# The opening of a decoder layer's kernel: constant matmuls before the first operands, first affines in halves, sums of operands behind the next modulation

## The chip, the cores and the metric

The kernel runs on one core of a Trainium2 chip. The metric is the device time of one launch in microseconds; three runs of the kernel before have a median of 1798.16 us.

## The reference, cut to what matters

One layer of a decoder with D = S = 1024: two gated feed-forward blocks (macaron halves) around a token mix, each behind a modulation by a vector c and before a LayerNorm. The change lies in the first block:

```python
silu_c = jax.nn.silu(c)
mods = silu_c @ w_ada[l] + b_ada[l]
sh1, sc1, g1, sh2, sc2, g2, sh3, sc3, g3 = [m[:, None, :] for m in jnp.split(mods, N_MODS, axis=-1)]
h = modulate(x, sh1, sc1)          # x * (1 + scale) + shift
y = swiglu(h, ffn1_w_gate[l], ffn1_w_up[l], ffn1_w_down[l])
```

The feed-forward width is 2816, so gate and up have 22 blocks of 128 columns each.

## The kernel before, in words

All matrices are f32. A product of f32 accuracy is made of three matmuls on halves (`split`, L101 to L103): ScalarE casts the operand to a high half (L102), VectorE subtracts it and leaves the low half (L103); `mm3` (L105 to L109) multiplies high by high, high by low, and low by high, each matmul 128 columns of weights against 512 columns.

The opening is `start_ffn1` (L561 to L633). The modulated input is made in eight chunks d of 128 features, transposed, 1024 tokens wide. `fetch(d)` loads two 128x1024 pieces of the modulation's weights (rows of adaT) and one chunk of x. `modulation(d)` (L579) reduces each piece against silu(c) on VectorE (`ada_mul`, L120: one reduction of 128x1024 and a short read of its accumulator) into a shift and a scale per feature. ScalarE applies them to the whole chunk (L597, 128x1024), then both token halves are split. TensorE multiplies the chunk at once with the weights of the first two column blocks of gate and of up, eight banks of PSUM wide (24 matmuls per chunk); these are the groups mm, mm, mm, o and y, y, tp, tp. After the last chunk ScalarE and VectorE evict the eight banks (L626 to L628: a Tanh, a scalar_tensor_tensor and a multiplication, four on VectorE for each of two row tiles).

The further column blocks are made by Strassen's scheme in the form of Winograd: seven products instead of eight (`product`, L280), over sums of the operands. T1 to T4 are sums of the input's quarters (`t_sum`, L221, on VectorE; `t_split`, L240), made of chunks d - 4 and d once chunk d is there, so in the rounds d of 4 to 7. Weights are loaded, summed and split in `w_ops` (L248). The seven products of gate, then of up, run in `gate_up` (L347).

A scheduler of the framework sets the order in which the instructions stand on each engine when the program is built: it starts what it holds to be ready earliest, within the order of the program. Each engine then works strictly in that order and waits on semaphores. `tc.issue_after(ins)` is a block whose instructions the scheduler places behind the instruction named. Buffers of SBUF are rings by tag (`RING`), and a load waits on SyncE's queue until a buffer is free. SyncE issues all loads and stores.

Of the kernel before, what the change touches and what calls it, by code (L numbers as in the profile page):

```python
# [1 line left out]

# [30 lines left out]
TAIL = 2  # L33
LOOK = 1
SECOND = 3
EARLY = 3
RATIO = 1.25
RATIO2 = 0.3
# [8 lines left out]
def layer_kernel(ctx, tc, xT, x, c, adaT, adab, wg1, wu1, wd1, wqk, wv1, wv2, bf, sinks,  # L47
# [16 lines left out]
    def st(tag, shape, dt=F32):  # L64
        assert 4 * math.prod(shape[1:]) <= RING[tag][1], (tag, shape)
        return mk(sb, shape, dt, tag, RING[tag][0])
# [7 lines left out]
    def psum(tag):  # L74
        return mk(ps, [P, HT], F32, tag, BANK[tag])
# [21 lines left out]
    def mod_b(m):  # L97
        return bcol[:, m * KD:(m + 1) * KD]
# [12 lines left out]
    def halves(t):  # L111
        return [t[:, :HT], t[:, HT:]]
# [7 lines left out]
    def ada_mul(w, j):  # L120
        m = j // KD
        s = 0.125 if m in (2, 8) else 0.5
        V.tensor_tensor_reduce(w, w, silu, scale=s, scalar=bcol[:, j:j + 1], op0=ALU.mult,
                               op1=ALU.add, accum_out=modc[:, j:j + 1])

    def ada_block(m, d):
        j = m * KD + d
# [112 lines left out]
    def t_split(n, ops, d):  # L240
        if n not in ops:
            ops[n] = htiles()
        split(ops[n][0][:, d], ops[n][1][:, d], ops["s" + n, d])
# [285 lines left out]
    for n in range(2):  # L529
# [2 lines left out]
        th = st("t", [P, HT])  # L532
        A.activation(th, silu[:, cs], AF.Tanh, scale=0.5)
        V.scalar_tensor_tensor(silu[:, cs], th, 1.0, silu[:, cs], op0=ALU.add, op1=ALU.mult)
    DMA.dma_start(bcol, adab)
    for m in (1, 4, 7, 2, 5, 8):
        V.tensor_scalar(mod_b(m), mod_b(m), 1.0, 0.25 if m in (2, 8) else 1.0, op0=ALU.add, op1=ALU.mult)

    def weight_std(w, c, tag):

# [20 lines left out]
    def start_ffn1():  # L561
        ops = {}
        hd = []
        blk = {}
        w0 = w1 = None
        p0 = [[psum("mm"), psum("mm")], [psum("mm"), psum("o")]]
        p1 = [[psum("y"), psum("y")], [psum("tp"), psum("tp")]]
        ada = {}

        def fetch(d):  # L570
            if d < KD:
                ada[d] = st("h", [P, 2, D])
                for m in range(2):
                    j = m * KD + d
                    DMA.dma_start(ada[d][:, m], adaT[j * P:(j + 1) * P, :])
                hd.append(st("z" if d < 4 else "q", [P, S]))
                DMA.dma_start(hd[d], xT[d * P:(d + 1) * P, :])

        def modulation(d):  # L579
            if d < KD:  # L580
                for m in range(2):
                    ada_mul(ada[d][:, m], m * KD + d)

        fetch(0)
        modulation(0)
        for d in range(KD):
            t = hd[d]
            if d:
                fetch(d + 1)
            if d in (0, SECOND):  # L590
                if d == 0:
                    w0 = [weight_std(wg1, 0, "w"), weight_std(wu1, 0, "w")]
                for _, load in w0:
                    load(d > 0)
            if d == 0:
                fetch(1)
            A.activation(t, t, AF.Identity, bias=modc[:, d:d + 1], scale=modc[:, KD + d:KD + d + 1])  # L597
            if d % 4 == 0:
                for hf in range(2):
                    blk[d // 4, hf] = htiles()  # L600
            for hf in range(2):
                hi, lo = blk[d // 4, hf]
                split(hi[:, d % 4], lo[:, d % 4], halves(t)[hf])
            if d in (0, SECOND):
                if d == 0:
                    w1 = [weight_std(wg1, 1, "w"), weight_std(wu1, 1, "t")]
                for _, load in w1:
                    load(d > 0)
            modulation(d + 1)
            for w, p in ((w0, p0), (w1, p1)):  # L610
                for q in range(2):
                    for hf in range(2):
                        hi, lo = blk[d // 4, hf]
                        mm3(p[q][hf], *w[q][0][d], hi[:, d % 4], lo[:, d % 4], d == 0, d == KD - 1)
            if d >= 4:
                for n in ("T1", "T2", "T3", "T4"):
                    t_sum(n, hd, ops, d - 4, V)
                for n in ("T1", "T2"):
                    t_split(n, ops, d - 4)
        ops["B11"], ops["B21"], ops["B22"] = blk[0, 0], blk[1, 0], blk[1, 1]  # L620
        a = []
        for j, p in enumerate((p0, p1)):
            a.append(st("z", [P, S]))
            for hf in range(2):
                t = halves(a[j])[hf]
                A.activation(t, p[0][hf], AF.Tanh, scale=0.5)  # L626
                V.scalar_tensor_tensor(t, t, 1.0, p[0][hf], op0=ALU.add, op1=ALU.mult)
                V.tensor_tensor(t, t, p[1][hf], ALU.mult)  # L628
        wo = w_ops(wg1, 2)
        for n in ("T3", "T4"):  # L630
            for d in range(4):
                t_split(n, ops, d)
        return ops, wo, a  # L633
# [7 lines left out]
    DMA.dma_start(gaincol, gain)  # L641
    DMA.dma_start(bfb, bf[0].partition_broadcast(P))
    DMA.dma_start(sinkb, sinks[0].partition_broadcast(P))
    V.memset(ones, 1.0)
    V.memset(nhalf, -0.5)
    V.tensor_scalar(nsink, sinkb, -1.0, None, op0=ALU.mult)

    rest = [(m, d) for m in range(2, 9) for d in range(KD)]
# [779 lines left out]
```

## Time and profile before

| | us |
|---|---|
| median of three runs | 1798.16 |
| lowest, highest | 1797.49, 1800.76 |
| the profiled execution | 1802.0 |
| its span, first to last instruction | 1800.2 |

PE is TensorE, PEld its weight loads, DVE VectorE, ACT ScalarE, SP SyncE. A row of a timeline says when an instruction starts, how long it takes from start to result, its line, operation and shape, and in brackets how long the engine had been idle before it and what ended that. Instructions overlap on an engine: the next one can start before the one before has its result, so what an instruction takes of the engine's time is read from the distance of starts. [...]

### The profile page before, as it was taken

Reading aid. Unit: us, or ns where it says so; the run is one execution under the profiler, and the core shown is the slowest. Engines: PE = TensorE matmul, PEld = TensorE weight load, DVE = VectorE, ACT = ScalarE, POOL = GpSimd, SP = SyncE. Lnnn points to the kernel's source line nnn. Section 1 sums busy time; section 2 is a strip of 40 time slices with the busy share of each in tenths; the row PEclk is TensorE's granted clock in tenths of the full one; section 3 lists DMA queues with packets and bytes.
Section 4 is the critical chain, followed back from the end, with each engine's and each line's share of the span. In section 5 each row is a group of like instructions: output and inputs, shape, how many; then the busy total and the mean of one; then the engine's idle time right before and its main releaser. Section 6 shows DMA issues by size and latency. Waiting matters only on the chain.

```text
span 1800.2 us, 23514 instructions
## 1 busy us (share of the span) xinstructions
PE 1749.5 (97%) x8114; PEld 1439.8 (80%) x8114; DVE 1520.0 (84%) x2759; ACT 772.3 (43%) x1481; POOL 23.1 (1%) x32
## 2 busy tenths in 40 slices
PE   7999999999999999999999989999999999999997
PEld 5788888888888889777777768678888888888885
DVE  7999999999696796378878887999788887789788
ACT  5433333333544452376556641543233333344472
POOL 0000000000000000000000000000000000000000
PEclk9999999999999999999999999999999999999999
DMA  9355565557944336755677862333224233593452
GB/s 366 122 193 180 192 200 183 185 175 250 324 122 146 94 102 224 228 154 161 187 212 214 231 221 85 130 111 135 94 94 137 92 105 100 189 314 112 136 163 82
DMA packets 147047, 303.44 MB, mean 169 GB/s; under 512 B 15384, under 2 KB 29296, under 8 KB 146928
## 3 DMA queue, kind: packets, MB, share of 16 engines
q1 hardware_dynamic: 146928, 301.94, 51.9%
q8 instruction: 64, 1.05, 0.3%
q14 instruction: 55, 0.45, 0.1%
HBM read 224.17 MB, written 77.71 MB: 168 GB/s over the span
## 4 chain that ended last, share of the span: by engine, by line
PE 80%; DVE 11%; ACT 3%; DMA 3%; issue 2%; POOL 0%; SPq 0%; ACTq 0%; DVEq 0%; POOLq 0%
PE y L107 11%; PE y L108 11%; PE y L109 11%; PE mm L107 9%; PE mm L109 9%; PE mm L108 9%; PE o L107 3%; PE o L108 3%; PE o L109 3%; DVE h L103 2%; PE tp L107 2%; PE tp L109 2%; PE tp L108 2%; DVE w L103 1%; PE tp L1140 1%
## 5 line engine op out<-in xcount | busy, mean ns | idle before, releaser
L102 ACT CAST w<-u 128x512 fp32r<-128x512 f32 x303 | 186.4, 622 | 387.6 <-PE y L109 156.9
L107 PE MATMUL y<-h,w 128*128 128x512 f32 x728 | 287.8, 395 | 5.1 <-ACT h L102 2.1
L108 PE MATMUL y<-h,w 128*128 128x512 f32 x728 | 286.1, 393 | 0.0
L109 PE MATMUL y<-h,w 128*128 128x512 f32 x728 | 285.6, 393 | 0.0
L103 DVE TENSOR_TENSOR w<-u,w 128x512 fp32r<-128x512 f32 x303 | 206.1, 685 | 25.0 <-ACT w L102 23.9
L107 PE MATMUL mm<-h,w 128*128 128x512 f32 x528 | 207.2, 393 | 18.6 <-ACT h L102 15.5
L108 PE MATMUL mm<-h,w 128*128 128x512 f32 x528 | 207.2, 393 | 0.3 <-DVE h L103 0.2
L109 PE MATMUL mm<-h,w 128*128 128x512 f32 x528 | 206.8, 392 | 0.0
L107 PEld LDWEIGHTS y<-h,w 128*128 128x128 f32 x728 | 137.2, 188 | 33.7 <-ACT h L102 2.5
L109 PEld LDWEIGHTS y<-h,w 128*128 128x128 f32 x728 | 137.1, 188 | 26.9
L108 PEld LDWEIGHTS y<-h,w 128*128 128x128 f32 x728 | 137.1, 188 | 25.8
L102 ACT CAST w<-t 128x512 fp32r<-128x512 f32 x106 | 65.5, 621 | 190.8 <-PE mm L109 68.8
L107 PEld LDWEIGHTS mm<-h,w 128*128 128x128 f32 x528 | 99.8, 189 | 40.7 <-ACT h L102 15.9
L108 PEld LDWEIGHTS mm<-h,w 128*128 128x128 f32 x528 | 100.2, 190 | 22.0 <-DVE h L103 1.5
L109 PEld LDWEIGHTS mm<-h,w 128*128 128x128 f32 x528 | 99.9, 189 | 21.5 <-DVE w L103 0.8
L102 ACT CAST z<-u 128x512 fp32r<-128x512 f32 x88 | 54.7, 622 | 93.1 <-PE y L109 59.8
L103 DVE TENSOR_TENSOR t<-tp,t 128x512 fp32r<-128x512 f32 (+1 forms) x126 | 72.9, 586 | 21.6 <-ACT t L102 20.3
L103 DVE TENSOR_TENSOR z<-u,z 128x512 fp32r<-128x512 f32 x88 | 60.1, 686 | 26.2 <-ACT z L102 26.1
L102 ACT CAST t<-tp 128x512 fp32r<-128x512 f32 (+1 forms) x126 | 62.3, 502 | 46.2 <-PE tp L1140 45.3
L102 ACT CAST w<-h 128x512 fp32r<-128x512 f32 x111 | 68.3, 617 | 31.8 <-DMA h<-in_wd 13.3
L103 DVE TENSOR_TENSOR w<-h,w 128x512 fp32r<-128x512 f32 x111 | 75.7, 685 | 5.3 <-ACT w L102 5.2
L103 DVE TENSOR_TENSOR w<-t,w 128x512 fp32r<-128x512 f32 x106 | 72.6, 687 | 1.6 <-ACT w L102 1.1
(347 smaller groups left out, 3909.3 us busy)
## 6 DMA issues: line engine op xcount, KB each, us to landing
u<-aT SPq DMA_DIRECT2D x154, 256.0 KB, 2.8
q<-in_adaT SPq DMA_DIRECT2D x56, 512.0 KB, 3.4
u<-in_wg SPq DMA_DIRECT2D x92, 256.0 KB, 3.0
u<-in_wu SPq DMA_DIRECT2D x90, 256.0 KB, 2.8
aT<-z SPq DMA_DIRECT2D x44, 512.0 KB, 3.4
h<-in_wd SPq DMA_DIRECT2D x88, 256.0 KB, 5.4
qkd<-w SPq DMA_DIRECT2D x26, 512.0 KB, 3.5
aT<-b SPq DMA_DIRECT2D x22, 512.0 KB, 4.2
```

Of the source, the lines that this page charges most:

```text
L102: A.copy(hi, src)
L103: V.tensor_tensor(lo, src, hi.bitcast(F32), ALU.subtract)
L107: T.matmul(o, lh, rh, start=start, stop=False, skip_group_check=more)
L108: T.matmul(o, lh, rl, start=False, stop=False, skip_group_check=more)
L109: T.matmul(o, ll, rh, start=False, stop=stop, skip_group_check=more)
L1140: T.transpose(pt[:, tok(i - q0)], sps[i][:, tok(j)], ident)
```

## The change

1. 28 matmuls of the constant `ones` with itself (128x128, f32) into a bank that nobody reads stand at the start of `start_ffn1`; the memsets of `ones` and `nhalf` move to the front for it, and the banks of the groups are asked for behind it.
2. The affine of chunks 0 and 1 is issued as two halves of 128x512.
3. The four sums and the two splits of a round d of 4 to 7 are placed behind the second reduction of `modulation(d + 1)`; after the last chunk there is none.
4. The load of the bias `bcol` is issued behind the first piece of the modulation's weights; of the six additions to it the one that the first scale needs stays ahead of the first modulation, and five are issued at the end of round 1.

```diff
@@ -1,3 +1,4 @@
+import contextlib
 import math
 
 import concourse.bass as bass
@@ -33,6 +34,7 @@
 TAIL = 2
 LOOK = 1
 SECOND = 3
+WARM = 28
 EARLY = 3
 RATIO = 1.25
 RATIO2 = 0.3
@@ -120,8 +122,8 @@
     def ada_mul(w, j):
         m = j // KD
         s = 0.125 if m in (2, 8) else 0.5
-        V.tensor_tensor_reduce(w, w, silu, scale=s, scalar=bcol[:, j:j + 1], op0=ALU.mult,
-                               op1=ALU.add, accum_out=modc[:, j:j + 1])
+        return V.tensor_tensor_reduce(w, w, silu, scale=s, scalar=bcol[:, j:j + 1], op0=ALU.mult,
+                                      op1=ALU.add, accum_out=modc[:, j:j + 1])
 
     def ada_block(m, d):
         j = m * KD + d
@@ -532,9 +534,13 @@
         th = st("t", [P, HT])
         A.activation(th, silu[:, cs], AF.Tanh, scale=0.5)
         V.scalar_tensor_tensor(silu[:, cs], th, 1.0, silu[:, cs], op0=ALU.add, op1=ALU.mult)
-    DMA.dma_start(bcol, adab)
-    for m in (1, 4, 7, 2, 5, 8):
-        V.tensor_scalar(mod_b(m), mod_b(m), 1.0, 0.25 if m in (2, 8) else 1.0, op0=ALU.add, op1=ALU.mult)
+
+    def bcol_add(ms):
+        for m in ms:
+            V.tensor_scalar(mod_b(m), mod_b(m), 1.0, 0.25 if m in (2, 8) else 1.0, op0=ALU.add, op1=ALU.mult)
+
+    V.memset(ones, 1.0)
+    V.memset(nhalf, -0.5)
 
     def weight_std(w, c, tag):
 
@@ -563,8 +569,6 @@
         hd = []
         blk = {}
         w0 = w1 = None
-        p0 = [[psum("mm"), psum("mm")], [psum("mm"), psum("o")]]
-        p1 = [[psum("y"), psum("y")], [psum("tp"), psum("tp")]]
         ada = {}
 
         def fetch(d):
@@ -573,16 +577,24 @@
                 for m in range(2):
                     j = m * KD + d
                     DMA.dma_start(ada[d][:, m], adaT[j * P:(j + 1) * P, :])
+                    if d + m == 0:
+                        DMA.dma_start(bcol, adab)
                 hd.append(st("z" if d < 4 else "q", [P, S]))
                 DMA.dma_start(hd[d], xT[d * P:(d + 1) * P, :])
 
         def modulation(d):
             if d < KD:
-                for m in range(2):
-                    ada_mul(ada[d][:, m], m * KD + d)
-
+                return [ada_mul(ada[d][:, m], m * KD + d) for m in range(2)][1]
+
+
+        warm = psum("o")
+        for _ in range(WARM):
+            T.matmul(warm[:, :P], ones, ones, start=True, stop=True)
         fetch(0)
+        bcol_add((1,))
         modulation(0)
+        p0 = [[psum("mm"), psum("mm")], [psum("mm"), psum("o")]]
+        p1 = [[psum("y"), psum("y")], [psum("tp"), psum("tp")]]
         for d in range(KD):
             t = hd[d]
             if d:
@@ -594,7 +606,8 @@
                     load(d > 0)
             if d == 0:
                 fetch(1)
-            A.activation(t, t, AF.Identity, bias=modc[:, d:d + 1], scale=modc[:, KD + d:KD + d + 1])
+            for hs in [t] if d > 1 else halves(t):
+                A.activation(hs, hs, AF.Identity, bias=modc[:, d:d + 1], scale=modc[:, KD + d:KD + d + 1])
             if d % 4 == 0:
                 for hf in range(2):
                     blk[d // 4, hf] = htiles()
@@ -606,17 +619,20 @@
                     w1 = [weight_std(wg1, 1, "w"), weight_std(wu1, 1, "t")]
                 for _, load in w1:
                     load(d > 0)
-            modulation(d + 1)
+            done = modulation(d + 1)
             for w, p in ((w0, p0), (w1, p1)):
                 for q in range(2):
                     for hf in range(2):
                         hi, lo = blk[d // 4, hf]
                         mm3(p[q][hf], *w[q][0][d], hi[:, d % 4], lo[:, d % 4], d == 0, d == KD - 1)
             if d >= 4:
-                for n in ("T1", "T2", "T3", "T4"):
-                    t_sum(n, hd, ops, d - 4, V)
-                for n in ("T1", "T2"):
-                    t_split(n, ops, d - 4)
+                with tc.issue_after(done.ins) if done else contextlib.nullcontext():
+                    for n in ("T1", "T2", "T3", "T4"):
+                        t_sum(n, hd, ops, d - 4, V)
+                    for n in ("T1", "T2"):
+                        t_split(n, ops, d - 4)
+            if d == 1:
+                bcol_add((4, 7, 2, 5, 8))
         ops["B11"], ops["B21"], ops["B22"] = blk[0, 0], blk[1, 0], blk[1, 1]
         a = []
         for j, p in enumerate((p0, p1)):
@@ -641,8 +657,6 @@
     DMA.dma_start(gaincol, gain)
     DMA.dma_start(bfb, bf[0].partition_broadcast(P))
     DMA.dma_start(sinkb, sinks[0].partition_broadcast(P))
-    V.memset(ones, 1.0)
-    V.memset(nhalf, -0.5)
     V.tensor_scalar(nsink, sinkb, -1.0, None, op0=ALU.mult)
 
     rest = [(m, d) for m in range(2, 9) for d in range(KD)]
```

The order of the instructions shows what the scheduler makes of it.

**ScalarE, chunks 0 and 1.** In round 1 the weights w and t are those of the second pair of blocks, and z is the chunk of x. Before:

```order
L597 ACTIVATE z_105<-z_105,modc 128x1024
L102 CAST w_109<-u_113 128x512
L102 CAST h_127<-z_105 128x512
L102 CAST w_111<-u_117 128x512
L102 CAST h_129<-z_105 128x512
L597 ACTIVATE z_124<-z_124,modc 128x1024
L102 CAST w_135<-u_137 128x512
L102 CAST t_143<-u_141 128x512
```

And now:

```order
L610 ACTIVATE z_122<-z_122,modc 128x512 x2
L104 CAST w_135<-u_139 128x512
L104 CAST h_154<-z_122 128x512
L104 CAST w_137<-u_143 128x512
L104 CAST h_156<-z_122 128x512
L610 ACTIVATE z_150<-z_150,modc 128x512
L104 CAST w_162<-u_164 128x512
L104 CAST t_170<-u_168 128x512
L610 ACTIVATE z_150<-z_150,modc 128x512
L104 CAST h_154<-z_150 128x512
```

In chunk 0 both halves still stand ahead of the first cast; in chunk 1 the casts of the second weights stand between the halves.

**VectorE, around the modulation of chunk 6** (its weights are h_352 before and h_385 now; lines L231, L234, L237 before and L230 to L239 now are sums, L103 and L105 low halves). Before:

```order
L231 TENSOR_TENSOR t_389<-q_302,z_124 128x512
L103 TENSOR_TENSOR h_349<-t_340,h_348 128x512
L103 TENSOR_TENSOR h_306<-q_302,h_305 128x512
L103 TENSOR_TENSOR h_308<-q_302,h_307 128x512
L234 TENSOR_TENSOR z_124<-q_302,z_124 128x512
L237 TENSOR_TENSOR q_302<-q_302,t_389 128x512
L103 TENSOR_TENSOR h_345<-z_124,h_344 128x512
L103 TENSOR_TENSOR h_349<-t_389,h_348 128x512
L123 ISA h_352,modc<-h_352,b_75,bcol 128x1024
L123 ISA modc 128x1
L123 ISA h_352,modc<-h_352,b_75,bcol 128x1024
L123 ISA modc 128x1
```

And now:

```order
L233 TENSOR_TENSOR t_373<-q_281,z_122 128x512
L236 TENSOR_TENSOR z_122<-q_281,z_122 128x512
L239 TENSOR_TENSOR q_281<-q_281,t_373 128x512
L105 TENSOR_TENSOR h_378<-z_122,h_377 128x512
L105 TENSOR_TENSOR h_339<-q_335,h_338 128x512
L105 TENSOR_TENSOR h_382<-t_373,h_381 128x512
L105 TENSOR_TENSOR h_341<-q_335,h_340 128x512
L105 TENSOR_TENSOR h_378<-z_245,h_377 128x512
L125 ISA h_385,modc<-h_385,b_75,bcol 128x1024
L125 ISA modc 128x1
L105 TENSOR_TENSOR h_563<-z_122,h_562 128x512
L125 ISA h_385,modc<-h_385,b_75,bcol 128x1024
```

The sums of chunk 1 with chunk 5 have moved from ahead of the two reductions to behind them; those of chunk 0 with chunk 4 still stand ahead. The two reductions are no longer next to each other.

**VectorE and TensorE, from the last chunk to the first Strassen products** (z_480 and z_513, z_487 and z_520 are the evicted row tiles; w are weights of the products). VectorE before:

```order
L103 TENSOR_TENSOR w_502<-u_494,w_502 128x512
L267 TENSOR_TENSOR t_505<-u_498,u_500 128x512
L103 TENSOR_TENSOR h_530<-z_105,h_529 128x512
L268 TENSOR_TENSOR t_506<-t_505,u_494 128x512
L271 TENSOR_TENSOR u_498<-u_494,u_498 128x512
L627 SCALAR_TENSOR_TENSOR z_480<-z_480,mm_94 128x512
L627 SCALAR_TENSOR_TENSOR z_480<-z_480,mm_95 128x512
L628 TENSOR_TENSOR z_480<-z_480,mm_96 128x512
L628 TENSOR_TENSOR z_480<-z_480,o_97 128x512
L103 TENSOR_TENSOR w_509<-t_506,w_509 128x512
L103 TENSOR_TENSOR w_512<-u_496,w_512 128x512
L103 TENSOR_TENSOR w_515<-t_505,w_515 128x512
```

And now:

```order
L105 TENSOR_TENSOR h_382<-t_505,h_381 128x512
L643 SCALAR_TENSOR_TENSOR z_513<-z_513,mm_127 128x512
L643 SCALAR_TENSOR_TENSOR z_513<-z_513,mm_128 128x512
L644 TENSOR_TENSOR z_513<-z_513,mm_129 128x512
L644 TENSOR_TENSOR z_513<-z_513,o_130 128x512
L643 SCALAR_TENSOR_TENSOR z_520<-z_520,y_131 128x512
L643 SCALAR_TENSOR_TENSOR z_520<-z_520,y_132 128x512
L644 TENSOR_TENSOR z_520<-z_520,tp_133 128x512
L644 TENSOR_TENSOR z_520<-z_520,tp_134 128x512
L105 TENSOR_TENSOR w_535<-u_527,w_535 128x512
L269 TENSOR_TENSOR t_538<-u_531,u_533 128x512
L105 TENSOR_TENSOR h_563<-z_203,h_562 128x512
```

TensorE before, from the last matmuls of chunk 7:

```order
L108 MATMUL tp_101<-h_308,t_269 128x512
L109 MATMUL tp_101<-h_307,t_270 128x512
L107 MATMUL mm_609<-h_348,w_509 128x512
L108 MATMUL mm_609<-h_349,w_509 128x512
L107 MATMUL mm_660<-h_529,w_519 128x512
L108 MATMUL mm_660<-h_530,w_519 128x512
L107 MATMUL o_642<-h_344,w_515 128x512
L108 MATMUL o_642<-h_345,w_515 128x512
L109 MATMUL mm_609<-h_348,w_509 128x512
L107 MATMUL mm_609<-h_348,w_509 128x512
```

And now:

```order
L110 MATMUL tp_134<-h_341,t_302 128x512
L111 MATMUL tp_134<-h_340,t_303 128x512
L109 MATMUL y_625<-h_154,w_535 128x512
L110 MATMUL y_625<-h_155,w_535 128x512
L111 MATMUL y_625<-h_154,w_535 128x512
L109 MATMUL y_625<-h_154,w_535 128x512
L110 MATMUL y_625<-h_155,w_535 128x512
L111 MATMUL y_625<-h_154,w_535 128x512
```

Before, four evictions stand behind the sums of the weights, and TensorE begins six matmuls of three products before it takes up one in full. Now all eight evictions stand ahead of the first low half of weights (w_535), and TensorE begins with product 1 on the bank y.

Behind some 580 matmuls the order is the same in both kernels on every engine.

## Rows read from the trace of the kernel before

**Rows 1.** The page, totals of the engines.

```profile
PE 1749.5 (97%) x8114; PEld 1439.8 (80%) x8114; DVE 1520.0 (84%) x2759; ACT 772.3 (43%) x1481; POOL 23.1 (1%) x32
```

**Rows 2.** Stages: length, busy us of PE, PEld, DVE, ACT, POOL; granted clock, DMA share, GB/s.

```profile
12.83:19.03 6.20, 5.85 (x12) 3.67 (x13) 4.99 (x10) 2.79 (x5) 0.00 (x0) 1.00 1.03 404
19.03:48.87 29.84, 29.84 (x131) 24.70 (x132) 28.81 (x48) 17.20 (x27) 0.00 (x0) 1.00 0.96 366
48.87:51.89 3.02, 0.39 (x2) 0.00 (x1) 3.02 (x6) 1.91 (x3) 0.00 (x0) 1.00 0.07 26
...
52.70:56.40 3.70, 3.70 (x11) 2.89 (x10) 3.70 (x8) 3.41 (x5) 0.00 (x0) 0.54 0.00 0
56.40:64.40 8.00, 8.00 (x37) 6.51 (x35) 7.67 (x14) 4.21 (x9) 0.00 (x0) 1.00 0.00 1
64.40:69.90 5.50, 4.68 (x20) 3.16 (x19) 5.50 (x10) 3.03 (x7) 0.00 (x0) 1.00 0.18 51
...
100.00:700.00 600.00, 600.00 (x2762) 502.54 (x2761) 543.94 (x908) 230.89 (x401) 5.25 (x8) 1.00 0.56 182
```

**Rows 3.** Waits of TensorE up to 700 us: total, times, longest.

```profile
PE mm L107 <- ACT h L102: 15.5, 2, 12.8
PE mm L107 <- ACT w L102: 0.6, 1, 0.6
PE y L107 <- ACT w L102: 0.3, 1, 0.3
```

**Rows 4.** Timeline of VectorE, 49 to 61 us: start us, us, what.

```profile
49.83 0.08 DVE L123 DVE_READ_ACCUMULATOR2_ANT modc<- 128x1 f32 x1
...
50.44 1.27 DVE L123 CUSTOM_DVE_ANT_0 h<-h,b,bcol 128x1024 f32<-128x1024 f32 x1
...
52.85 0.08 DVE L123 DVE_READ_ACCUMULATOR2_ANT modc<- 128x1 f32 x1
...
54.05 0.68 DVE L231 TENSOR_TENSOR t<-q,z 128x512 f32<-128x512 f32 x1
...
60.08 0.68 DVE L103 TENSOR_TENSOR h<-t,h 128x512 fp32r<-128x512 f32 x1
```

**Rows 5.** Timeline of VectorE, the first instruction.

```profile
0.83 0.17 DVE L644 MEMSET ones<- 128x128 f32 x1 [0.83 <-PEq L1420]
```

**Rows 6.** Timeline of TensorE, the matmuls with f32 weights near 985 us.

```profile
984.59 1.84 PE L904 MATMUL tp<-ones,b 128*128 128x1 f32 x16
```

**Rows 7.** Timeline of TensorE, 12 to 68 us.

```profile
14.23 0.63 PE L109 MATMUL mm<-h,w 128*128 128x512 f32 x1
...
18.07 0.63 PE L109 MATMUL o<-h,w 128*128 128x512 f32 x1
19.03 0.50 PE L107 MATMUL y<-h,w 128*128 128x512 f32 x1 [0.33 <-ACT w L102]
...
51.89 0.73 PE L107 MATMUL mm<-h,w 128*128 128x512 f32 x2 [2.63 <-ACT h L102]
...
64.31 0.39 PE L109 MATMUL tp<-h,t 128*128 128x512 f32 x1
...
66.22 0.50 PE L107 MATMUL mm<-h,w 128*128 128x512 f32 x1 [0.58 <-ACT w L102]
```

**Rows 8.** Timeline of ScalarE, the second chunk.

```profile
17.23 1.24 ACT L597 ACTIVATE z<-z,modc 128x1024 f32<-128x1024 f32 x1 [3.41 <-DVE modc L123]
18.38 0.60 ACT L102 CAST w<-u 128x512 fp32r<-128x512 f32 x1
18.88 0.62 ACT L102 CAST t<-u 128x512 fp32r<-128x512 f32 x1
```

**Rows 9.** Timeline of VectorE, the second group of weights begins.

```profile
34.16 0.69 DVE L234 TENSOR_TENSOR z<-q,z 128x512 f32<-128x512 f32 x1 [0.71 <-ACT q L597]
34.77 1.89 DVE L103 TENSOR_TENSOR w<-u,w 128x512 fp32r<-128x512 f32 x3
```

**Rows 10.** Timeline of SyncE's queue, the last modulation weights.

```profile
32.88 6.09 SPq L575 DMA_DIRECT2D h<-in_adaT  x4
```


## The prediction

> **What bounds the kernel now.** I read the totals first, then the stages, then who waits. TensorE is busy for 1749.5 of 1800.2 us [rows 1]. From 100 to 700 us it is busy for all 600.00 us [rows 2], so whatever time the opening gains or loses is carried, microsecond for microsecond, into everything behind it. The change touches the opening alone: behind some 140 us both kernels have the same instructions in the same order on every engine. So the question is when the first products of the Strassen part run.
>
> The stages [rows 2] show the losses there. Nothing runs on TensorE before 12.83 us. The first 12 matmuls fill the 6.20 us to 19.03. Until 48.87 it never stops: 29.84 of 29.84 us, 131 matmuls, 0.228 us each. Then it has 0.39 us of work in 3.02 us, and from 52.70 to 56.40 it runs at a granted clock of 0.54. From 64.40 to 69.90 it is busy for 4.68 of 5.50 us. The waits [rows 3] name the causes: 15.5 us for the high halves of the operands, which ScalarE casts (12.8 us of it the start), 0.6 and 0.3 us for casts of weights.
>
> What stands behind these waits is VectorE. It works 28.81 of 29.84 us and then without a pause [rows 2]. An ordinary instruction of 128x512 takes 0.603 us of its time (ten steps from 54.05 to 60.08 us), one reduction of a modulation 1.205 us (two from 50.44 to 52.85) [rows 4].
>
> **The change part by part.** *Constant matmuls.* 28 products of a 128x128 f32 tile with itself, from the memset of that tile (done at 1.00 us [rows 5]) on. The trace has no such matmul; the nearest row has 8 matmuls with the same f32 weights, one column wide, recorded as 16 and taking 1.84 us [rows 6], 0.23 us each. At the higher level that is 6.4 us, at the lower about twice, 12.9 us: they end between 7.4 and 13.9 us. [...] But the thirteenth needs a cast of the second weights, and waits for it already now, until 19.03 [rows 3, 7]. So I cost the faster clock at nothing: that cast covers it. If the constants end at 13.9 us, they delay the first operands by 1.1 us, which the same cover takes up.
>
> *Affines in halves.* For the first chunk both halves stand ahead of the first cast, so nothing moves. For the second, ScalarE now casts the second weights behind half an affine. Today the affine of 128x1024 starts at 17.23 and the cast at 18.38 us; a piece of 128x512 takes 0.50 us there (18.38 to 18.88) [rows 8]. So this cast starts some 0.6 us earlier, and with it the subtraction of VectorE behind it and the whole alternation of modulation, affine and cast up to the fifth chunk. **Gain 0.6 us**, on the path. The first weight subtraction of the second group, now at 34.77 us, moves to about 34.1: 0.6 us from this, 0.1 from the sum that stood before it [rows 9].
>
> *Sums behind the modulation.* Nothing is removed: VectorE has the same work in another order. Three of the four early sums (0.603 us each) stood ahead of 34 us, beside waits for casts; they move behind it, where VectorE doesn't wait. I count the new order of VectorE from that weight subtraction on, ordinary instructions at 0.603 and reductions at 1.205 us.
> - The modulation of chunk 6 is complete behind 16 ordinary instructions and 4 reductions: 34.1 + 9.6 + 4.8 + 0.08 = 48.6 us, against 49.91 now [rows 4]. TensorE's first matmul on it came 1.98 us later (51.89 [rows 7]); in the new order ScalarE has one other cast (0.5 us) in between, so now at 51.1. TensorE ends chunk 5 about 0.9 us earlier than now (0.6 above, 0.3 of the old wait at 19.03). **The gap of 2.63 us [rows 7] stays.**
> - The last low half of chunk 7 starts behind 32 ordinary instructions and 6 reductions: 34.1 + 19.3 + 7.2 = 60.6. TensorE then finishes chunk 7 at about 64.5, where it does today (64.31 + 0.39 [rows 7]).
> - Now the loss. Today TensorE goes on with products whose weights were prepared ahead of the evictions: two of their matmuls follow at once, and the third runs at 66.22 [rows 7]. In the new order product 1 comes first. It needs a bank that the fifth eviction frees, and its third matmul needs the low half of its weights, which stands behind all eight evictions. The fifth eviction starts behind 41 ordinary instructions and 6 reductions: 34.1 + 24.7 + 7.2 = 66.0, done at 66.7. The low half stands behind 45 and 6: 34.1 + 27.1 + 7.2 = 68.4, done 0.68 later [rows 4], and with 0.05 us to the next engine (18.38 + 0.60 to 19.03 [rows 7, 8]) the third matmul runs at 69.2. Today the matmul of the same place, the third behind chunk 7, runs at 66.22. **Loss 3.0 us**, with the gain of 0.6 already in it. That VectorE waits somewhere in this count would add some tenths; ScalarE should have its casts ready, as it works only 4.21 of 8.00 us there [rows 2].
>
> *The clock.* Between 64.6 and 69.2 us TensorE has two matmuls. In the kernel before, after 3.02 us with 0.39 of work and 0.81 us more, the clock fell for 3.70 us [rows 2]; that costs 3.70 x (1 - 0.228/0.427) = 1.7 us. It did not fall between 64.40 and 69.90, with 4.68 of 5.50 busy. The new stretch is nearer to the first, so I take the fall, and 1.4 us of it, since some waits for casts of weights would have been there anyway. Ends: 0 (the clock holds), and 2.9 us (low as long as at the start, 6.20 us). The fall at 52.70 stays in my count, and there VectorE covers it.
>
> *Small ones.* The first half of the modulation's weights is issued ahead of the bias, one bias instruction pair stands before the first reduction, four behind the second: within 0.3 us, and covered by the same cast. On SyncE two weight loads now pass ahead of the last four loads of modulation weights, which were issued from 32.88 us on, over 6.09 us [rows 10]; by my count the first of them is wanted at 45.6 us only, so this costs nothing.
>
> **Sum:** +3.0 + 1.4 = +4.4 us. The profiled execution took 1802.0 us (span 1800.2), 3.8 more than the median of the runs; by its own time this makes 1806.4, by the median of 1798.16 it makes **1802.6 us**, 0.24% slower. About 0.2%, or 3.6 us, is what can be told from no change here.
>
> **The rivals.** *The clock holds.* The same loss of 3.0 us without the fall: 1801.2. For it: two matmuls stand in the middle of the stretch. Against: the row of 3.02 us. *Longer low clock*: +5.9, so 1804.1.
>
> *The opening follows TensorE.* If VectorE reaches the modulation of chunk 6 before TensorE ends chunk 5 (48.3 us), the gap of 2.63 us closes, TensorE keeps its 0.9 us, and the result is 3.5 us faster, 1794.7. It is decided where the count reads 48.6 us for that modulation: it would have to be at 45.8, which leaves 11.7 us instead of 14.5 for the same instructions. Against it, VectorE works without a pause in that stretch [rows 2]; and the products' weights would still be behind the evictions.
>
> [...]
>
> *Nothing to see*: the reordering costs as much as the earlier start gives, 1798.2.
>
> **How the numbers follow.** Forecast (loss and fall) 0.52, clock holds 0.24, longer fall 0.08, opening follows TensorE 0.06, start pays 0.04, nothing 0.06. The range takes in both slower cases and the equal one: from 1798.0 to 1806.0, where the upper end is +5.9 with the spread of the three runs shown (1797.49 to 1800.76) on top. Slower by over 0.2% are the forecast in three quarters of its cases, the longer fall and a fifth of the held clock, together 0.52; faster by over 0.2% is half of the two fast rivals with a little for what I don't see, 0.07; the rest, 0.41, is within 0.2%.
>
> **What would show it.** Right: the wait of TensorE near 51 us is still there; about 64.5 us it stops for about 2 us, runs two matmuls, stops again for about 2 us until a low half of weights from VectorE; the clock is low in the stretch behind; from 100 us on nothing has changed but the origin. The first 12 matmuls step by 0.23 us, and TensorE then stands still until about 18.4. Wrong: if the low half of product 1 is ready before 67 us, or if TensorE has no gap between chunks 5 and 6, my count of VectorE fails, and with it the sign.

## The result, and the profile after

| | median us | lowest, highest | runs |
|---|---|---|---|
| before, beside it | 1800.76 | 1797.49, 1803.50 | 5 |
| changed | 1808.54 | 1806.08, 1812.73 | 5 |

The ratio is 1.0047, with an interval from 1.0034 to 1.0059: slower, by 6 to 11 us. The forecast was 1802.6, its range 1798.0 to 1806.0: the sign was right, the size was not. The profiled execution took 1808.54 us, with a span of 1806.8 (1800.2 before).

The totals of the changed kernel; TensorE has 56 instructions more, the 28 constant products, of two records each:

```profile
PE 1760.3 (97%) x8170; PEld 1449.6 (80%) x8170; DVE 1520.9 (84%) x2759; ACT 774.1 (43%) x1483; POOL 23.1 (1%) x32
```

Its stages, with the columns of [rows 2]; the granted clock is TensorE's, as a share of full speed:

```profile
13.24:19.02 5.78, 5.42 (x12) 3.61 (x12) 4.39 (x9) 2.36 (x5) 0.00 (x0) 0.59 1.03 405
19.02:49.30 30.28, 30.27 (x132) 24.70 (x132) 27.51 (x46) 15.72 (x24) 0.00 (x0) 1.00 0.94 358
49.30:51.69 2.39, 0.00 (x1) 0.00 (x0) 2.39 (x7) 2.31 (x4) 0.00 (x0) 1.00 0.00 0
51.69:55.90 4.21, 4.18 (x10) 2.95 (x11) 4.21 (x8) 2.55 (x5) 0.00 (x0) 0.59 0.00 0
55.90:65.39 9.49, 9.21 (x39) 6.80 (x38) 9.42 (x17) 7.54 (x14) 0.00 (x0) 1.00 0.01 3
65.39:70.00 4.61, 0.74 (x4) 0.30 (x3) 4.61 (x9) 0.94 (x2) 0.00 (x0) 0.92 0.00 0
70.00:76.11 6.11, 6.11 (x15) 4.84 (x15) 6.11 (x11) 2.29 (x5) 0.00 (x0) 0.50 0.35 129
76.11:100.00 23.89, 23.89 (x107) 19.77 (x106) 21.21 (x37) 9.39 (x16) 0.00 (x0) 1.00 0.63 210
100.00:700.00 600.00, 600.00 (x2750) 501.87 (x2749) 542.57 (x907) 232.07 (x401) 5.23 (x8) 1.00 0.57 183
```

From 100 to 700 us TensorE never stops, as before, so the loss lies in the opening. The stretch with 4.68 of 5.50 us busy [rows 2] has become one with 0.74 of 4.61, and behind it come 6.11 us at a granted clock of 0.50. VectorE works through all of both.

The waits of TensorE up to 700 us, with the columns of [rows 3]:

```profile
PE mm L109 <- ACT h L104: 6.5, 2, 4.1
PE y L109 <- DVE z L643: 2.2, 1, 2.2
PE y L111 <- DVE w L105: 1.7, 1, 1.7
```

The first line is the start and the gap at chunk 6; the other two are new. TensorE's timeline shows them at product 1, bank y:

```profile
65.01 0.39 PE L111 MATMUL tp<-h,t 128*128 128x512 f32 x1
67.60 0.50 PE L109 MATMUL y<-h,w 128*128 128x512 f32 x1 [2.21 <-DVE z L643]
67.94 0.40 PE L110 MATMUL y<-h,w 128*128 128x512 f32 x1
70.00 0.80 PE L111 MATMUL y<-h,w 128*128 128x512 f32 x1 [1.66 <-DVE w L105]
70.59 0.63 PE L109 MATMUL y<-h,w 128*128 128x512 f32 x1
...
75.71 0.56 PE L110 MATMUL y<-h,w 128*128 128x512 f32 x1
76.11 0.40 PE L109 MATMUL o<-h,w 128*128 128x512 f32 x1
```

Two matmuls stand alone between two stops, and from 70.59 to 75.71 the steps are 0.427 us (12 of them in 5.12 us) instead of 0.228. VectorE in the same stretch:

```profile
66.27 0.68 DVE L644 TENSOR_TENSOR z<-z,o 128x512 f32<-128x512 f32 x1
66.86 1.28 DVE L643 SCALAR_TENSOR_TENSOR z<-z,y 128x512 f32<-128x512 f32 x2
68.06 1.28 DVE L644 TENSOR_TENSOR z<-z,tp 128x512 f32<-128x512 f32 x2
69.25 0.69 DVE L105 TENSOR_TENSOR w<-u,w 128x512 fp32r<-128x512 f32 x1
```

The fifth eviction starts at 66.86 and frees the bank; the low half of product 1's weights (w at 69.25) stands behind all eight.

Below, three times place a loss. **F** is the first matmul on operands. **T** is the third matmul behind chunk 7, the one of [rows 7] at 66.22. **M** is the first transposition of a modulation column on TensorE, which has the same number of matmuls on operands ahead of it in every kernel here; TensorE works without a stop from 100 us to it. F is the start, T - F what VectorE's order and the waits cost, M - T what the clock and the waits behind T cost. M before and after, in TensorE's timeline:

```profile
447.44 0.27 PE L136 MATMUL tp<-ident,modc 128*8 128x128 f32 x1
```

```profile
453.59 0.27 PE L138 MATMUL tp<-ident,modc 128*8 128x128 f32 x1
```

The change in M, 6.15 us, is nearly all of the 6.6 us by which the span grew. In the table, the time and its ratio to the kernel before beside it come from all runs, and F, T and M from one profiled run each.

| | median us | before | ratio (95%) | F | T - F | M - T | M |
|---|---|---|---|---|---|---|---|
| before | | | | 12.83 | 53.39 | 381.22 | 447.44 |
| changed | 1808.54 | 1800.76 | 1.0047 (1.0034 to 1.0059) | 13.24 | 56.76 | 383.59 | 453.59 |
| E1 order undone | 1802.25 | 1800.18 | 1.0009 (1.0000 to 1.0017) | 13.03 | 52.95 | 381.20 | 447.18 |
| E2 no constants | 1806.52 | 1800.18 | 1.0033 (1.0020 to 1.0046) | 12.73 | 56.76 | 382.38 | 451.87 |
| E3 filler | 1803.07 | 1800.18 | 1.0016 (1.0006 to 1.0025) | 12.73 | 56.76 | 381.08 | 450.57 |
| E4 weights first | 1806.96 | 1800.18 | 1.0037 (1.0023 to 1.0051) | 12.96 | 55.57 | 382.48 | 451.01 |
| E5 whole affines | 1806.49 | 1800.72 | 1.0030 (1.0020 to 1.0041) | 12.56 | 57.18 | 383.08 | 452.82 |
| E6 order alone | 1806.39 | 1800.72 | 1.0032 (1.0021 to 1.0043) | 13.32 | 57.19 | 383.58 | 454.09 |
| E7 sums on GpSimd | 1813.44 | 1800.72 | 1.0073 (1.0061 to 1.0085) | 12.98 | | | 459.15 |
| E8 the same, banks | 1811.01 | 1800.72 | 1.0065 (1.0051 to 1.0080) | 13.35 | | | 457.98 |
| E9 weights first, banks | 1806.82 | 1800.35 | 1.0029 (1.0018 to 1.0040) | 12.96 | 53.79 | 384.97 | 451.72 |
| E10 38 constants | 1804.95 | 1800.35 | 1.0025 (1.0016 to 1.0034) | 12.95 | 56.74 | 383.00 | 452.69 |
| E11 bias in front | 1807.34 | 1800.35 | 1.0030 (1.0018 to 1.0042) | 13.19 | 56.75 | 382.32 | 452.26 |
| E12 halves alone | 1799.65 | 1800.35 | 0.9995 (0.9987 to 1.0004) | 13.05 | 52.95 | 381.18 | 447.18 |
| E13 changed again | 1806.92 | 1801.26 | 1.0038 (1.0025 to 1.0050) | 13.17 | 56.76 | 382.69 | 452.62 |

Behind M the profiled spans hold between 1350.4 us (E8) and 1356.4 us (E7): 1352.8 before, 1353.2 in the changed kernel, 1352.1 in E1 and 1355.7 in E12. This spread goes with no part of the change, so a single time can move by several us for reasons that don't lie in the opening, and M is the finer measure of it.

### The profile page after: what moved, and what is told of

It is laid out like the page before. It is cut to its first block, busy times and chain, and to the rows that moved or that the text cites. A ratio compares the mean times of both kernels' runs of the same rounds, so it can differ in the third digit from the quotient of the medians.

```text
span 1806.8 us, 23633 instructions
## 1 busy us (share of the span) xinstructions
PE 1760.3 (97%) x8170; PEld 1449.6 (80%) x8170; DVE 1520.9 (84%) x2759; ACT 774.1 (43%) x1483; POOL 23.1 (1%) x32
## 4 chain that ended last, share of the span: by engine, by line
PE 81%; DVE 11%; ACT 3%; DMA 2%; issue 2%; POOL 0%; SPq 0%; ACTq 0%; DVEq 0%; POOLq 0%
PE y L109 11%; PE y L111 11%; PE y L110 11%; PE mm L110 9%; PE mm L111 9%; PE mm L109 9%; PE o L111 3%; PE o L110 3%; PE o L109 3%; PE tp L111 2%; PE tp L109 2%; PE tp L110 2%; DVE h L105 2%; PE tp L1154 1%; PE o L1158 1%
## 5 line engine op out<-in xcount | busy, mean ns | idle before, releaser
L105 DVE TENSOR_TENSOR w<-u,w 128x512 fp32r<-128x512 f32 x303 | 206.6, 688 | 27.5 <-ACT w L104 26.4
L105 DVE TENSOR_TENSOR t<-tp,t 128x512 fp32r<-128x512 f32 (+1 forms) x126 | 73.0, 586 | 21.4 <-ACT t L104 20.4
L105 DVE TENSOR_TENSOR w<-h,w 128x512 fp32r<-128x512 f32 x111 | 76.7, 693 | 10.4 <-ACT w L104 10.4
L105 DVE TENSOR_TENSOR z<-u,z 128x512 fp32r<-128x512 f32 x88 | 61.3, 699 | 23.8 <-ACT z L104 23.8
L105 DVE TENSOR_TENSOR w<-t,w 128x512 fp32r<-128x512 f32 x106 | 73.2, 693 | 2.7 <-ACT w L104 2.3
```

The source lines that it names most:

```text
L105: V.tensor_tensor(lo, src, hi.bitcast(F32), ALU.subtract)
```

## The experiments

**E1, the order undone.**

```diff
-                with tc.issue_after(done.ins) if done else contextlib.nullcontext():
+                with contextlib.nullcontext():
```

> The changed kernel with its sums and splits no longer held behind the modulation (the block without the ordering). Theory A, the order alone made the loss: product 1's weights then stand ahead of the evictions again, the stop at 67.6 to 70.0 us and the low clock behind it go, and the time falls by 4 to 7 us, to 1801.5 to 1804.5. Theory B, the new start (constant matmuls, late bias) made it: the time stays at 1808.5 within 1. Theory C, the wait was harmless and the clock is low behind chunk 7 anyway: 2 to 3 us back, 1806.

TensorE's timeline behind chunk 7, without the ordering:

```profile
64.07 0.39 PE L111 MATMUL tp<-h,t 128*128 128x512 f32 x1
64.70 0.47 PE L109 MATMUL mm<-h,w 128*128 128x512 f32 x1 [0.23 <-DVE z L643]
65.00 0.40 PE L110 MATMUL mm<-h,w 128*128 128x512 f32 x1
65.98 0.50 PE L109 MATMUL mm<-h,w 128*128 128x512 f32 x1 [0.58 <-ACT w L104]
```

These are the waits of the kernel before again [rows 7], and the matmuls behind them step by 0.23 us, at a granted clock of 1.00 from 64 to 78 us. The time falls by 6.3 us against the changed kernel's first measurement and 4.7 against its second (E13). The order is the loss. The 2.1 us by which E1's median still lies above the kernel before, with an interval that begins at 1.0000, are not in the opening: M is 447.18 against 447.44.

**E6, the order alone, in the kernel before** (its `ada_mul` and `modulation` hand on the last reduction, as in the change).

```diff
-            modulation(d + 1)
+            done = modulation(d + 1)
...
+                with tc.issue_after(done.ins) if done else contextlib.nullcontext():
```

> The kernel before with the sums and splits placed behind the modulation as the only change; no constant matmuls, whole affines, bias in front. Theory A (the order makes the whole loss): the stops ahead of product 1 and of its third matmul are there, the third matmul runs at about 70, the clock falls behind it, and the transposition of the modulation (447.44 us in the kernel before, 453.59 in the changed one) comes at 452 to 454; the time is 1805.5 to 1809, the same as of the changed kernel. Theory B (the new start has a part in it): 1801 to 1804.

1806.39, M 0.1 us past the expected 454. T - F grows from 53.39 to 57.19: the order costs 3.80 us there. From E1 to the changed kernel it is 56.76 - 52.95 = 3.81.

**E3, a filler for the stop.** 16 constant matmuls behind the first evictions.

```diff
                 V.tensor_tensor(t, t, p[1][hf], ALU.mult)
+                if j == 0 and hf == 0:
+                    warm = psum("mm")
+                    for _ in range(16):
+                        T.matmul(warm[:, :P], ones, ones, start=True, stop=True)
```

> The changed kernel with 16 more constant matmuls between chunk 7 and product 1, into the bank that the first eviction frees; at 0.289 us each they fill 4.6 us of the stop at 65.4 to 70.0 us. Theory A, the 14 matmuls behind the stop at 0.427 us are a cost of their own of 14 x 0.2 = 2.8 us: the clock stays up, the third matmul of product 1 still comes at about 70, and the time falls by 2 to 3 us, to 1805.5 to 1806.5. Theory C, what follows is bound by VectorE and the low clock is covered: 1808.5 within 0.7. If the filler does not hold the clock: 1808.5 as well, with steps of 0.427 us behind it.

TensorE's timeline with the filler:

```profile
64.73 3.81 PE L648 MATMUL mm<-ones 128*128 128x128 f32 x32
68.30 0.48 PE L109 MATMUL y<-h,w 128*128 128x512 f32 x1
68.61 0.40 PE L110 MATMUL y<-h,w 128*128 128x512 f32 x1
69.49 0.50 PE L111 MATMUL y<-h,w 128*128 128x512 f32 x1 [0.48 <-DVE w L105]
69.82 0.40 PE L109 MATMUL y<-h,w 128*128 128x512 f32 x1
```

T - F is the same 56.76, since VectorE is as late as without the filler; but the steps stay at 0.23 us (granted clock 1.00 from 69.49 to 76.11 us), and M - T returns to 381.08. That separates the two terms: the wait costs 56.76 - 53.39 = 3.4 us, the halves' gain in it, and the clock costs what M - T has above 381.2, 2.4 in the changed kernel. The steps give the same: 12 of them at 0.427 instead of 0.228 us are 2.4 us. The time, 1803.07, fell by more than the expected 2 to 3 us from 1808.54, and by 3.9 from E13; but each against the kernel before beside it, the loss is 2.9 us with the filler and 5.7 (E13) without. M - T falls by 1.6 (from E13) to 2.5 us (from the first profile): about 2 us is what the clock was worth.

**E4 and E9, what product 1 waits for.** E4 asks for the products' weights ahead of the evictions; E9 also exchanges the banks of the groups, so that the first eviction frees bank y.

```diff
+        wo = w_ops(wg1, 2)
         a = []
         for j, p in enumerate((p0, p1)):
...
-        wo = w_ops(wg1, 2)
```

```diff
-        p0 = [[psum("mm"), psum("mm")], [psum("mm"), psum("o")]]
-        p1 = [[psum("y"), psum("y")], [psum("tp"), psum("tp")]]
+        p0 = [[psum("y"), psum("y")], [psum("tp"), psum("tp")]]
+        p1 = [[psum("mm"), psum("mm")], [psum("mm"), psum("o")]]
```

> The changed kernel with the weights of the first seven products asked for ahead of the evictions instead of behind them. Theory A: product 1 no longer waits for its low half, only for its bank, which comes 5 ordinary VectorE instructions later than before, and the third matmul runs some 1 to 1.5 us earlier than 70.0; the stop in one piece instead of two still lets the clock fall: 1806.5 to 1808. If the wait for the low half was the whole loss: 1803 to 1804.

> The run with the weights ahead of the evictions, and with the banks of the two groups exchanged, so that the first eviction frees the bank of product 1: both things that product 1 waited for in the changed kernel come early. Theory A (VectorE is what is late, whichever product comes first): the third matmul of product 1 runs some 53.5 us behind the first matmul on operands instead of 56.8, but TensorE then waits 2.5 to 3 us for the next product's bank or weights, and gains 0.5 to 1 us in all, with 0 to 2.5 us of low clock as the fall may be in two short pieces or none; the transposition of the modulation at 450 to 452.5, the time 1803.5 to 1806.5. Rival (the wait of product 1 is the whole loss): no wait behind it, no fall, the transposition at 447 to 448, the time 1800 to 1801.5.

E4 moved T 1.2 us forward, the expected amount, and the clock still fell, to a mean of 0.82 from 70 to 78 us. The way was another than expected. TensorE now begins with a product on bank mm, and its first wait is not for a bank but for a cast of weights:

```profile
67.38 0.50 PE L109 MATMUL mm<-h,w 128*128 128x512 f32 x1 [2.27 <-ACT w L104]
...
68.53 0.50 PE L111 MATMUL mm<-h,w 128*128 128x512 f32 x1 [0.42 <-DVE w L105]
```

In E9 product 1 runs early and whole, and the next product waits:

```profile
66.21 0.47 PE L109 MATMUL y<-h,w 128*128 128x512 f32 x1 [1.10 <-DVE z L644]
...
68.82 0.39 PE L111 MATMUL y<-h,w 128*128 128x512 f32 x1
71.62 0.59 PE L109 MATMUL y<-h,w 128*128 128x512 f32 x1 [2.41 <-ACT w L104]
```

ScalarE's cast that ends this wait had itself waited for a sum of VectorE:

```profile
70.91 1.14 ACT L104 CAST w<-u 128x512 fp32r<-128x512 f32 x2 [2.02 <-DVE u L275]
```

M - F is 438.76, against 439.45 (E13) and 440.35. Product 1 was not the whole loss: VectorE is what is late, and a wait taken away turns up at the next product. The time, 1806.82, came out 0.3 us above what I expected.

**E2, E10, E11, the start.** E2: `WARM = 0`; E10: `WARM = 38`; E11: the bias and its six additions in front again.

```diff
-WARM = 28
+WARM = 38
```

```diff
     V.memset(nhalf, -0.5)
+    DMA.dma_start(bcol, adab)
+    bcol_add((1, 4, 7, 2, 5, 8))
...
-                    if d + m == 0:
-                        DMA.dma_start(bcol, adab)
...
-        bcol_add((1,))
...
-            if d == 1:
-                bcol_add((4, 7, 2, 5, 8))
```

> The changed kernel without the 28 constant matmuls, nothing else. Theory A: they neither help nor harm, since the first operands come 4.1 us after the last of them and TensorE's thirteenth matmul waits for a cast in any case: 1808.5 within 0.7, first matmuls still stepping by 0.427 us. Theory B, the constants delay the start or heat the chip: 1802 to 1805. A third possibility, they do save clock time at the start: 1810 to 1811.

> The changed kernel with 38 constant matmuls instead of 28, so that they end at about 12 to 13.5 us, where the first operands come. Theory A: the clock may stay up, and the first 12 matmuls on operands then step by 0.23 us and end by 16.2, but the thirteenth waits for the cast of the second weights some 2 us, and from there on all is at the same distance from the first matmul on operands (the third matmul of product 1 at 56.8 us): no gain, 1806 to 1809. Rival (the clock at the start is worth something): that distance falls by 1 to 2 us.

> The changed kernel with the load of the bias and its six additions in front again. Theory A: nothing of it is on the path; the first matmul on operands at 12.6 to 13.4 us as in all runs so far, and the third matmul of product 1 at 56.8 us behind it: 1806 to 1809. Rival (the late bias holds up the first modulations): both 0.3 to 0.5 us earlier.

T - F is 56.76, 56.74 and 56.75: nothing of the start reaches T. E2's time, 1806.52, lies below the band of its Theory A and above that of Theory B; both had been set from 1808.54, and beside 1806.92 (E13) it shows no difference. Its first matmuls step by 0.427 us although the clock's column reads 1.00 there, as in the kernel before; in the changed kernel the same step stands beside 0.59. So at the start I go by the steps and not by the column. With 38 constants TensorE's start looks as the prediction had described it for 28:

```profile
1.05 11.19 PE L592 MATMUL o<-ones 128*128 128x128 f32 x76 [1.05 <-DVE nhalf L543]
12.95 0.50 PE L109 MATMUL mm<-h,w 128*128 128x512 f32 x1 [0.71 <-ACT h L104]
...
15.94 0.39 PE L110 MATMUL o<-h,w 128*128 128x512 f32 x1
16.17 0.39 PE L111 MATMUL o<-h,w 128*128 128x512 f32 x1
18.72 0.50 PE L109 MATMUL y<-h,w 128*128 128x512 f32 x1 [2.17 <-ACT w L104]
```

The granted clock is 1.00 from 13 to 19 us, the steps are 0.23 us, and the 2 us saved are waited away at the cast of the second weights. The stages of this run behind that wait, columns as in [rows 2]:

```profile
18.72:22.00 3.28, 3.28 (x10) 2.61 (x11) 3.28 (x6) 2.21 (x4) 0.00 (x0) 0.67 1.02 405
22.00:24.00 2.00, 2.00 (x8) 1.58 (x7) 2.00 (x4) 0.35 (x1) 0.00 (x0) 0.69 1.01 401
```

The clock falls behind this stop too, to a mean of 0.67 and 0.69; TensorE then reaches chunk 6 later, and its gap there is 0.83 us instead of 2.4, so T doesn't move. E10's median of 1804.95 is below what I expected, and 2 us below E13; beside their own kernels before the two are 4.6 and 5.7 us slower, with intervals that overlap. The opening gives no reason (M 452.69 against 452.62), but the profiled execution, at 1807.08, was the slowest of the ten runs, so a gain of about 1 us in the others isn't ruled out.

**E5 and E12, the halves.** E5 takes them out of the changed kernel, E12 puts them alone into the kernel before.

```diff
-            for hs in [t] if d > 1 else halves(t):
-                A.activation(hs, hs, AF.Identity, bias=modc[:, d:d + 1], scale=modc[:, KD + d:KD + d + 1])
+            for hs in [t]:
+                A.activation(hs, hs, AF.Identity, bias=modc[:, d:d + 1], scale=modc[:, KD + d:KD + d + 1])
```

> The changed kernel with the affine of chunks 0 and 1 whole again, nothing else. The prediction counted 0.6 us for the halves, through the cast of the second weights. Theory A (that gain is real and was hidden in the comparison by a later start of 0.4 us in the profiled run): measured from the first operand matmul, the wait for the cast of the second weights grows from 0.3 us to about 0.9, the first weight subtraction of the second group and everything behind it up to product 1 come some 0.5 us later; the time is 1808.5 to 1810. Rival (the halves gave nothing): the same distances from the first operand matmul as in the changed kernel, within 0.1 us.

> The kernel before with the affines of chunks 0 and 1 in halves as the only change: the part that I hold to be a gain, without the order. The third matmul behind chunk 7, now 53.4 us behind the first matmul on operands, comes at 52.9 to 53.0, as in the run without the ordering; the transposition of the modulation at 446.7 to 447.4; 0.4 us is 0.02% and can't be told from no change by the time, 1799.5 to 1801 if the kernel before is at 1800.5.

T - F: 57.18 without them and 56.76 with them; 53.39 and 52.95 in the kernel before. They gain 0.43 us, too little to be seen in a time. E5's time, 1806.49, missed its band of 1808.5 to 1810, which again had been set from 1808.54. ScalarE's timeline of the changed kernel, at the second chunk, shows why it is 0.43 and not 0.6:

```profile
17.65 0.81 ACT L610 ACTIVATE z<-z,modc 128x512 f32<-128x512 f32 x1 [3.42 <-DVE modc L125]
18.37 0.60 ACT L104 CAST w<-u 128x512 fp32r<-128x512 f32 x1
```

Half an affine takes 0.72 us of ScalarE's time, where a cast of the same shape takes 0.50; the whole one takes 1.15 [rows 8], and 1.15 - 0.72 = 0.43.

**E7 and E8, a version meant to win.** If VectorE is the bound, GpSimd, idle there, could take the 16 sums. Both are E1 with

```diff
-                        t_sum(n, hd, ops, d - 4, V)
+                        t_sum(n, hd, ops, d - 4, G)
```

and E8 has the banks of E9 besides.

> The changed kernel without the ordering and with the 16 sums of the operands on GpSimd, which is idle in the opening, instead of VectorE. If VectorE's work is what bounds the opening (my count), 16 x 0.603 = 9.6 us less on it shorten both stops: the first matmul on chunk 6 some 0.8 us earlier than 51.7, the products behind chunk 7 without a stop of note, the transposition of the modulation 2.5 to 4 us earlier than in the run without the ordering (447.2), at 443 to 445, the time 1796.5 to 1799.5. This supposes at most 1.5 us for a sum on GpSimd. Rival: GpSimd takes 3 us and more for one, or holds VectorE up while it works: 1802 or more.

> The run with the sums on GpSimd, and with the banks of the two groups exchanged, so that the first eviction frees the bank of product 1. If the bank is what product 1 still waits for, another 0.4 to 0.7 us on the opening; if the weights of the product are, nothing.

M comes 12 us later than in E1 (E8: 10.8), and the theory of a free engine fell. The banks of E8 gave 1.2 us on M, more than the 0.4 to 0.7 expected. VectorE's timeline in E7:

```profile
58.67 0.68 DVE L105 TENSOR_TENSOR h<-z,h 128x512 fp32r<-128x512 f32 x1
59.27 1.27 DVE L125 CUSTOM_DVE_ANT_0 h<-h,b,bcol 128x1024 f32<-128x1024 f32 x1
...
64.96 1.77 DVE L105 TENSOR_TENSOR h<-t,h 128x512 fp32r<-128x512 f32 x1
66.66 1.77 DVE L269 TENSOR_TENSOR t<-u,u 128x512 f32<-128x512 f32 x1
68.36 1.76 DVE L105 TENSOR_TENSOR h<-z,h 128x512 fp32r<-128x512 f32 x1
```

and GpSimd's:

```profile
60.10 1.59 POOL L233 TENSOR_TENSOR t<-q,z 128x512 f32<-128x512 f32 x1 [4.91 <-ACT q L610]
...
64.58 1.60 POOL L239 TENSOR_TENSOR q<-q,t 128x512 f32<-128x512 f32 x1 [0.69 <-DVE h L105]
66.15 1.74 POOL L233 TENSOR_TENSOR t<-q,z 128x512 f32<-128x512 f32 x1
67.84 1.73 POOL L236 TENSOR_TENSOR z<-q,z 128x512 f32<-128x512 f32 x1
```

While GpSimd sums, in these rows VectorE's instructions come every 1.70 us instead of 0.603: each sum taken off saves VectorE 0.6 us and costs an instruction beside it 1.1.

**E13, the changed kernel again.** No edit.

> The changed kernel as it is, measured again. If the opening is the whole difference: 5 to 6.5 us above the kernel before, so 1805 to 1807, like the variants that keep the order (1804.95 to 1807.34), with the third matmul of product 1 56.8 us behind the first matmul on operands and 7 to 14 matmuls at 0.427 us behind it. If something further back in the change costs time too: again 7 to 8.5 us above.

5.7 us above the kernel beside it, as the opening alone would have it (M + 5.2). The 7.8 us of the first comparison hold some 1.5 to 2 us of spread between measurements.

## Why the prediction was wrong in size and right in sign

Two terms of the sum failed. The base, 1798.16 us, stood 2.6 us below what the kernel before measured beside the changed one, and the low clock behind the stops, put at 1.4 us, cost 2.4. The mechanism held.

- **Constants.** They end at 9.13 us, within 7.4 to 13.9. The first matmuls then did not step by 0.23 us but by 0.427 until 17.64: TensorE was idle for 4.11 us in between, and from 13.24 to 19.02 the granted clock is 0.59. That sign failed. The same 28 constants took 7.9 to 9.3 us in other runs, and steps of 0.23 us began between 16.7 us (E3) and 19.5 (E13); T - F is 56.76 in both. The price of nothing, because the cast of the second weights covers it, was right (E2, E10).
- **That the start pays** got a chance of 0.04, and it didn't. In E10 the granted clock is 1.00 from 13 to 19 us and the first matmuls step by 0.23 us instead of 0.427, which would be 2.4 us for 12 of them and 1795.8 from the base of 1798.16. T - F is 56.74 beside 56.76, and the time is 1804.95.
- **Halves.** 0.6 us counted, 0.43 measured; the cast was the path, as said. The count priced half an affine like a cast, 0.50 us instead of 0.72.
- **Order of VectorE.** The mechanism, the place and both waits were as predicted, in the order predicted: bank, two matmuls, low half. T was put 3.0 us later with the halves' gain in it; measured from F it is 56.76 - 53.39 = 3.37. The first weight subtraction of the second group stands 21.43 us behind F where 21.3 was counted, and T 35.33 us behind it where 35.1 was counted. The gap at chunk 6 stayed (2.39 us).
- **Clock behind it.** This term was mis-sized. "I take the fall, and 1.4 us of it": the profiled run has 383.59 - 381.22 = 2.4. In the other runs whose T - F is about 57, without the filler, the same difference is 1.1 (E11), 1.2 (E2), 1.5 (E13), 1.8 (E10), 1.9 (E5) and 2.4 (E6), so the price is no constant. 1.4 lies low in that span, and the profiled run's 2.4 is nearer to the 2.9 of the rival with the longer low clock, which got a chance of 0.08; 2.9 held them all. The 0.427 us in these prices is the step of the kernel before at its start (14.23 to 18.07 us, nine steps [rows 7]). That the clock was low there no run of that kernel shows, as its column reads 1.00; in the changed kernel the same step stands beside 0.59 at the start and 0.50 behind the stops.
- **The low clock behind the gap at chunk 6** was rightly counted as covered. In E5 and E10 the clock did not fall there (granted 1.00 from 50 to 64 us; in the changed kernel's first profile 0.57 from 52 to 56). From its first matmul on chunk 6 to 64 us TensorE was idle for 1.22 us instead, and T - F stayed: 57.18 in E5 beside 57.19 in E6, both with whole affines, and 56.74 in E10 beside 56.76.
- **Start.** F came 0.41 us later than in the profile of before. Among all fifteen profiles F lies between 12.56 and 13.35, with and without each part of the change: spread, for which the sum had no term.
- **The base, the step that cost most.** "By the median of 1798.16 it makes 1802.6." Three runs gave 1798.16; beside the changed kernels the kernel before stood at 1800.18 to 1801.26, with up to 25 runs. Against the profiled execution's own 1802.0 the same sum gave 1806.4, and the changed kernel's second measurement is 1806.92; that nearness is in part luck, as 1802.0 is above every one of these medians and +4.4 is less than the 5.2 to 6.15 us that M grew.

The miss of 5.9 us against 1808.54 is then: base 1800.76 - 1798.16 = 2.6; clock 1.0; start 0.4; wait 0.4; and 7.8 - 6.15 = 1.6 of spread (6.0 by the rounding of the parts). The range's upper end was +5.9 on the same low base and 1.9 us for the spread, though the spread that it names is 2.6 and makes 1806.7; neither 1806.0 nor 1806.7 held either measurement.

Two things stay open. E1 and E12 have the same opening (M 447.18), yet ratios of 1.0009 and 0.9995; what makes the times spread behind M is not shown. And no version here beats the kernel before: E12 can't be told from it.

## What to carry to other kernels

Where an engine without slack feeds another, moving its work later changes nothing in its total (VectorE here: 1520.0 us before, 1520.9 after); ask what the waiting engine needs first after the move, and count the instructions now ahead of that. The stop here cost twice, 3.4 us as a wait and 1.1 to 2.4 us behind it, where the granted clock was lower and no later wait covered that; the second part differed from run to run. For an effect of 0.2% the base must be known to better than that: three runs were off by 0.14%.

## What the runs showed that I had not expected

GpSimd's 128x512 sums (1.3 to 2.2 us in E7, most of them 1.6 to 1.75) held up VectorE: in the rows of E7 above, its f32 instructions of the same size stand 1.70 us apart instead of 0.603. The periods of the two engines are nearly equal there (1.57 and 1.69 us between GpSimd's last three sums, 1.70 on VectorE). What makes them so is not shown.

The filler of E3 ran at 0.119 us a record (32 in 3.81 us), the constants at the start of the changed kernel at 0.144 (56 in 8.09 us). Why the start is slower is not shown.
